# Neighbourhood attention inside a two-layer diffusion step: where the first output products, the context scores and the last heads' steps stand in the row of TensorE

## The chip, the cores and the metric

One core of one Trainium2 chip runs the whole program in a single launch. The time is the device time of one execution in microseconds (us), and the smaller is the better. The kernel before the change took 1602.42 us in the median of three runs (1601.96 to 1604.28).

## What is computed

The reference is one inference step of a trunk with two layers, on 128 context tokens ("prompt") and 512 latent tokens of width 1024, laid out as a grid of 8 rows of 64. Each layer is a token mixer followed by a gated feed-forward network with a width-3 convolution. The mixer of layer 0 is neighbourhood attention with 16 heads of 64, that of layer 1 is grouped-query attention. All arithmetic is float32. The part that the change touches, cut to its core:

```python
def na_qkv(h, w_qkv):                       # one product, split into queries, keys, values
    q, k, v = jnp.split(h @ w_qkv, 3, axis=-1)
...
qp, kp, vp = na_qkv(hp, na_w_qkv[i])        # the 128 context tokens
op = blocked_attention(qp, kp, vp)          # context attends to itself only
...
qs, ks_, vs = na_qkv(hs, na_w_qkv[i])       # the 512 latent tokens
os_ = neighbourhood_attention(qs, ks_, vs, cache_na_k[:, i], cache_na_v[:, i], na_rpb[i])
...
xp = xp + g_ap * rmsnorm(op.reshape(bp, tp, -1) @ w_o, norm_mix_post[l])
xs = xs + g_as * rmsnorm(os_.reshape(bs, ts, -1) @ w_o, norm_mix_post[l])
```

In neighbourhood attention a latent query sees the latent keys of all 8 rows within a window of 16 columns, with a learned relative bias, and all 128 cached context keys, in one softmax.

## The kernel before, in words

**Precision.** Every operand of a product is split into a high and a low part (`wh`/`wl` for weights, `oh`/`ol`, `kh`/`kl`, and so on), and a product is three matmuls: high by high, low by high, high by low. The splitting is a cast on ScalarE (ACT) for the high part and a subtraction on VectorE (DVE) or GpSimd (POOL) for the low one.

**One order for TensorE.** The helpers `mm` and `turn` (lines 113 to 117) tie each matmul and transpose to the one before it, so TensorE (PE) runs exactly in the order in which the program is written. The other engines' instructions are put in order by a scheduler when the program is built. Each engine then works through its own list first in, first out.

**Head 0 to head 15.** `Head.scores(slot)` (line 900) makes the scores of one of four blocks of 128 latent queries of one head: two matmuls into a PSUM bank `s`, on DVE the table of biases added with the running minimum (line 910), on ACT the exponential into `p` (line 914), on DVE the reciprocal `rc` of its sum (line 917), and on POOL `p` times `rc` (line 918). `Head.turns(i)` (line 920) transposes four 128x128 blocks of `p` on PE into a bank `tp` and copies them out as `pk`. `turns(0)` needs blocks of all four slots: its first two transposes those of slots 0 and 1, its third and fourth those of slots 2 and 3. `values` (line 934) multiplies two heads' transposed probabilities with the values, into the bank `po`. The bias table `tb` of a head is built on POOL by three subtractions (line 875), two heads' tables being kept at a time.

For the 128 context tokens, `prompt_scores` (line 637) makes the scores of four heads at once (eight matmuls of 128x128 into `sp`), with their exponentials `pp` on ACT and the scaling on POOL (line 658). `prompt_turn` (line 661) transposes them and copies them out as `ptp` on ACT (line 666). This is done in heads 1, 5, 9 and 13 for the heads of their group of four.

**The stream of other products.** `work` is a generator (line 978, `stream`) of pieces of the query, key and value products of later heads; each `fill()` takes one piece, that is 6 matmuls `qk` or 6 to 9 `vp`. When a pair's last key product is in, `kp` is transposed and written out by `tail` (line 846, bank `tk`). After head 12 the stream is empty, and `early` (line 1067) puts another in its place: pieces of the mixer's output product, each one `Mix.part0(t, p)` (line 701): three matmuls `y` of 128x512 that add the contribution of head pair `p` to the first 512 output columns of token block `t`. Head pair `p` needs `oh`/`ol`, the split of the attention's result (`o_split`, line 958). The pairs 0 and 1 (`OEARLY` is 2) are split after head 11, the pairs 2 to 5 after head 12, and 6 and 7 behind that.

**The tables.** Which step follows which inside a head is written out by hand in `ORDER` and `ORDER2` (lines 49 to 56), read by the loop at line 1012. `ORDER[0]` serves the even heads up to 12, `ORDER[1]` the odd ones up to 11, and `ORDER2` the heads 13 (index 1), 14 and 15. In a table `f` takes the next piece of `work`, `t0` to `t2` are this head's transposes, `s0` to `s3` the scores of the next head, `v` the values of two heads, `p0` to `p2` the scores, transposes and values of the context (only in heads 1, 5, 9 and 13), and `a` a step of the adaLN rows. `PRO` (line 57) is the number of pieces that are done ahead of head 0's scores.

**After the last head** the remaining output products follow, their normalization, and the first feed-forward network (`ffn`, line 1098), then layer 1. Its up-projection's weights are partly sums and differences (`wr`, lines 1167 to 1170, on DVE), which are split by ACT and POOL (lines 1146 and 1147), and its convolution runs on DVE (line 1223) and ACT (line 1221).

Of the kernel before, what the change touches and what calls it, by code (L numbers as in the profile page):

```python
# [2 lines left out]

# [21 lines left out]
NT = T // P  # L25
# [17 lines left out]
OEARLY = 2  # L43
# [2 lines left out]
NC = 3  # L46
QKH = (slice(0, 256), slice(256, T))
CTX = 2
ORDER = (
    "f f t0 s0 f s1 t1 f f t2 f a f f s2 s3 f f f f f f".split(),  # L50
    "f f p0 t0 s0 f s1 t1 f t2 p1 f f f v a p2 s2 s3 f f f".split(),
)
ORDER2 = (
    "t0 s0 s1 f f f f t1 f f t2 f f f s2 f f s3 f f f".split(),
    "t0 p0 s0 s1 f f f f t1 t2 p1 f f f v p2 s2 f s3 f f".split(),
)
PRO = 19
PSTEP = (3, 5, 6, 6, 8, 9)
WU = 29
TP = 1  # L60
# [41 lines left out]
def hybrid_step(ctx: ExitStack, tc: tile.TileContext, A, O):  # L102
# [10 lines left out]
    def mm(*a, **k):  # L113
        pe(nc.tensor.matmul(*a, **k))  # L114

    def turn(*a, **k):
        pe(nc.tensor.transpose(*a, **k))  # L117
# [4 lines left out]
    def pool(name, bufs=1, side="left", **k):  # L122
        return tc.tile_pool(name=name, bufs=bufs, side=side, reuse_waits="tile", **k)
# [187 lines left out]
    def drain(gen):  # L311
        for _ in gen:
            pass
# [347 lines left out]
    def prompt_turn(ap, pp, tag, nb):  # L661
        tp = bk.get("tp")
        for i in range(4):
            turn(tp[:, i * P : i * P + P], pp[:, i, :], ident)
        x = ap.tile([P, 512], F32, tag=tag, name="ptp", bufs=nb)
        nc.scalar.copy(x, tp)
        bk.put(tp)
        return x.rearrange("p (a b) -> p a b", a=4)
# [71 lines left out]
    with l_na:  # L740
# [39 lines left out]
        def na_qk_items(p):  # L780
# [13 lines left out]
            def k_put(c0, c1, src):  # L794
                for b in range(2):
                    own, oth = own_oth(b)
                    nc.scalar.copy(d["kh"][b][own, c0:c1], src[own])
                    nc.scalar.copy(d["kh"][b][oth, c0:c1], src[own])
                    nc.vector.tensor_sub(d["kl"][b][own, c0:c1], src[own], f32(d["kh"][b][own, c0:c1]))

            def part(which, half, k0):
# [27 lines left out]
                else:  # L829
                    if half == 0:  # L830
# [3 lines left out]
                        turn(tk[:, 0:P], d["kc"], ident)  # L834
                        k_put(CTX * P, CTX * P + P, tk[:, 0:P])
                        bk.put(tk)
                    if half == 1:
                        d["kp"] = ap.tile([P, P], F32, tag="kc", name="kp", bufs=2)
                        nc.scalar.copy(d["kp"], pp[:, NS - cs.start : T - cs.start])
                    k0 = cs.start + P * (cs.start >= CTX * P)  # L840
                    k_put(k0, k0 + nq, pp[:, 0:nq])
# [92 lines left out]
        def values(two):  # L934

            po = bk.get("po")
            vt = vts_of[two[0].h // 4]

            def block(ov, c, x):
                for v in two:  # L940
                    rows_ = slice(64 * v.b, 64 * v.b + 64)
                    mm(ov[rows_], vt[:, c, v.h % 4, :], x(v), start=c == 5, stop=c == 3)

            block(po, 5, lambda v: v.t[0])
            for i in (1, 2):
                for a, c in enumerate(Head.BANKS[i]):
                    ov = po[:, c * P : c * P + 256] if c < 3 else po.rearrange("p (a b) -> p a b", b=P)[:, 0::3, :]
                    block(ov, c, lambda v: v.t[i][:, a * 256 : a * 256 + 256])
            om = of0[two[0].h // 2][:, 0:NS].rearrange("p (r c) -> p r c", c=GW)
            for c0, c1, q0 in ((8, 56, 128), (56, 64, 0), (0, 8, 64)):  # L950
                nc.scalar.copy(om[:, :, c0:c1].rearrange("p r c -> p c r"),
                               po[:, q0 : q0 + 8 * (c1 - c0)].rearrange("p (c r) -> p c r", r=8))
            bk.put(po)

        osp0 = []
        m0 = Mix(0, A["na_w_o"][0], lambda p, t: tuple(x[:, t * P : t * P + P] for x in osp0[p]))

        def o_split(p):
            hi, lo = osp0[p]
            nc.scalar.copy(hi, of0[p])  # L960
            nc.vector.tensor_sub(lo, of0[p], f32(hi))
# [16 lines left out]
        def stream():  # L978
            items[0][0]()
            tail = None  # L980
            for n, (load, parts) in enumerate(items):
                for i, part in enumerate(parts):
                    part()
                    if n + 1 == len(items) and i in OW:
                        m0.weights(0, OW[i], None if i == 4 else nc.gpsimd)
                    if i == 1 and n + 1 < len(items):
                        items[n + 1][0]()
                    if i == 4 and tail:
                        tail()
# [12 lines left out]
        def fill(n=1):  # L1002
            for _ in range(n):
                next(work, None)

        fill(PRO)
        next(ada0)
        head = Head(0)
        for slot in range(4):
            head.scores(slot)  # L1010
            fill()
        for h in range(H):
            nxt = Head(h + 1) if h + 1 < H else None
            g = h // 4
            pr = h % 4 == 1
            order = (ORDER if h < 13 else ORDER2)[h % 2]
            for i, step in enumerate(order):
                if step == "f":
                    if i < len(order) - 1 or h % 4 or not h:
                        fill()  # L1020
                elif step == "a":
                    next(ada0, None)
                elif step[0] == "s" and nxt:
                    nxt.scores(int(step[1]))
                elif step[0] == "t":
                    head.turns(int(step[1]))
                elif step == "v":
                    values((before, head))
                if pr and step == "p0":
                    sides = []  # L1030
                    for hh in range(4 * g, 4 * g + 4):
                        qs, kh, kl = qk_of[hh // 2]
                        b = hh % 2
                        sides.append((qs[b][:, QW - P :], kh[b][:, T:], kl[b][:, T:]))
                    pp = prompt_scores(ap, sides)
                if pr and step == "p1":
                    pth = prompt_turn(ap, pp, "pk", NPK)
                if pr and step == "p2":
                    po = bk.get("po")
                    for j in range(2):  # L1040
                        for b in range(2):
                            mm(po[64 * b : 64 * b + 64, j * P : j * P + P], vts_of[g][:, 4, 2 * j + b, :],
                               pth[:, 2 * j + b, :], start=True, stop=True)
                    for j in range(2):
                        nc.scalar.copy(of0[2 * g + j][:, NS:T], po[:, j * P : j * P + P])
                    bk.put(po)
            before = head
            head = nxt
            if h == 11:
                drain(ada0)  # L1050
                l_ada.close()
                epool = l_na.enter_context(pool("o0e", 1))
                osp0.extend([epool.tile([P, T], F32R, name=f"o{i}{p}") for i in "hl"] for p in range(OEARLY))
                for p in range(OEARLY):
                    o_split(p)
            if h == 12:
                drain(work)
                r_h0.close()
                hpool = r_na.enter_context(pool("o0h", 1, "right"))
                osp0.extend([hpool.tile([P, T], F32R, name=f"o{i}{p}") for i in "hl"] for p in range(OEARLY, KC))  # L1060
                for p in range(OEARLY, 4):
                    o_split(p)
                m0.weights(0, 3)
                for p in range(4, 6):
                    o_split(p)

                def early():
                    for ts in (range(2), range(2, NT)):
                        for p in range(6):
                            for t in ts:  # L1070
                                m0.part0(t, p)
                                yield

                work = early()
            if h == 13:
                o_split(6)
        drain(work)
# [781 lines left out]
```

## Time and profile before

One execution was profiled; its own time is 1601.92 us, with 1600.1 us of it in the span that the profile shows.

| What | Value |
|---|---|
| Median of three runs | 1602.42 us |
| Profiled execution, time / span | 1601.92 / 1600.1 us |
| Busy share of the span: PE, DVE, ACT, POOL | 96%, 64%, 54%, 44% |
| PE: matmuls, busy | 9709, 1537.8 us |
| Mean granted clock of PE | 0.983 of full speed |
| Neighbourhood attention, head 0's first scores to head 15's values | about 82.6 to 349.9 us |

A row of the list of waits reads: engine, destination and line, the instruction that released it, then the idle time in all, how many times, and the longest. A row of the timeline reads: start in us, length in us (neighbouring instructions with the same names are put together, with their count behind the x), engine, line, operation, destination and sources, shape, and in brackets the idle time of the engine just before it and what ended that. A matmul's length holds its passage through the array, so neighbouring rows overlap; the distance from start to start is what it takes in a row of them. In a table of windows, each row has the stretch, its length, the busy time and number of instructions of PE, of its weight loads, of DVE, ACT and POOL, then the granted clock of PE (1.00 is full speed), the share of time in which the DMA engines were busy, and GB/s.

### The profile page before, as it was taken

The numbers are of one execution on the slowest core, as the hardware profiler recorded it, in microseconds if no ns is written. First come the engines' busy times: TensorE is split into PE (matmuls) and PEld (weight loads), VectorE is DVE, ScalarE is ACT, GpSimd is POOL, SyncE is SP. The second block draws the span as 40 slices with busy tenths as digits, with TensorE's granted clock in tenths as the row PEclk, the third lists the DMA queues.
The fourth block names the chain that finished last, engine by engine and source line by source line (L and its number), as shares of the span: only waits on it lengthen the run. The fifth ranks groups of instructions, "written<-read, shape, count | busy, mean of one in ns | idle before, by whom it ended". The sixth has DMA issues, their size and how long they took to land.

```text
span 1600.1 us, 26043 instructions
## 1 busy us (share of the span) xinstructions
PE 1537.8 (96%) x9709; PEld 1357.3 (85%) x9709; DVE 1023.9 (64%) x1650; ACT 859.8 (54%) x1641; POOL 710.9 (44%) x609
## 2 busy tenths in 40 slices
PE   5999999899999999999999898999999999999998
PEld 3989899778999999988887676777899999998886
DVE  3453533638877666665656867773787888876454
ACT  3474655545555555554453536764656565565343
POOL 1654544423255445534444344441324655553433
PEclk8999999899999999999999998999999999999999
DMA  9745454227466566578573110003644333348664
GB/s 288 188 112 146 115 156 117 65 69 234 140 197 203 195 211 184 188 255 288 169 238 132 60 40 14 2 1 106 234 125 158 117 114 108 105 158 269 207 213 139
DMA packets 193210, 242.41 MB, mean 151 GB/s; under 512 B 11100, under 2 KB 149564, under 8 KB 193084
## 3 DMA queue, kind: packets, MB, share of 16 engines
q1 hardware_dynamic: 182224, 233.13, 45.4%
q10 hardware_dynamic: 10860, 7.62, 2.7%
q8 instruction: 76, 1.25, 0.3%
q14 instruction: 50, 0.41, 0.1%
HBM read 214.38 MB, written 26.34 MB: 150 GB/s over the span
## 4 chain that ended last, share of the span: by engine, by line
PE 55%; DVE 9%; POOL 5%; ACT 3%; issue 3%; DMA 1%; ACTq 0%; POOLq 0%; DVEq 0%
PE acc L114 18%; PE ux L114 15%; PE uz L114 6%; PE uy L114 4%; PE y L114 2%; PE s L114 2%; PE po L114 2%; PE tp L117 2%; PE ada L114 2%; POOL wl L1147 1%; DVE t L1223 1%; POOL vl L1147 1%; DVE al L1147 1%; POOL rh L1467 1%; DVE wl L167 1%
## 5 line engine op out<-in xcount | busy, mean ns | idle before, releaser
L167 POOL TENSOR_TENSOR wl<-wr,wh 128x1024 fp32r<-128x1024 f32 x74 | 183.1, 2476 | 261.7 <-ACT wh L165 252.3
L1147 POOL TENSOR_TENSOR wl<-wr,wh 128x1024 fp32r<-128x1024 f32 x76 | 183.5, 2437 | 39.5 <-ACT wh L1146 35.9
L114 PE MATMUL ux<-B,wh 128*128 128x322 f32 x832 | 199.9, 311 | 0.7 <-ACT u L1200 0.7
L1223 DVE SCALAR_TENSOR_TENSOR t<-C,cw,t 128x644 f32<-128x644 f32 x176 | 156.3, 888 | 56.0 <-ACT t L1221 55.6
L114 PE MATMUL acc<-wh,alo 128*128 128x512 f32 x440 | 172.3, 392 | 0.5 <-DVE alo L1116 0.5
L114 PE MATMUL acc<-wh,ahi 128*128 128x512 f32 x440 | 172.0, 391 | 0.0
L114 PE MATMUL acc<-wl,ahi 128*128 128x512 f32 x440 | 171.9, 391 | 0.0
L165 ACT CAST wh<-wr 128x1024 fp32r<-128x1024 f32 x140 | 145.3, 1048 | 40.7 <-DMA wr<-in_ffn_w_down 30.9
L114 PE MATMUL uz<-B,wh 128*128 128x322 f32 x640 | 156.2, 312 | 0.7 <-ACT v L1200 0.7
L114 PEld LDWEIGHTS ux<-B,wh 128*128 128x128 f32 x832 | 143.4, 189 | 3.2 <-ACT u L1200 1.0
L1116 DVE TENSOR_TENSOR alo<-ain,ahi 128x384 fp32r<-128x384 f32 (+1 forms) x88 | 80.3, 930 | 85.7 <-ACT ahi L1114 84.7
L114 PE MATMUL ux<-B,wl 128*128 128x322 f32 x416 | 129.3, 311 | 2.7 <-DVE wl L1147 2.7
L114 PE MATMUL qk<-hT,wh 128*128 128x384 f32 (+1 forms) x512 | 122.9, 317 | 0.1
L114 PEld LDWEIGHTS uz<-B,wh 128*128 128x128 f32 x640 | 111.2, 189 | 3.6 <-ACT vh L1146 1.6
L1221 ACT ACTIVATE t<-C,cw 128x644 f32<-128x644 f32 x88 | 78.6, 894 | 53.8 <-DVE C L1251 41.1
L1147 POOL TENSOR_TENSOR vl<-wr,vh 128x1024 fp32r<-128x1024 f32 x38 | 96.3, 2534 | 24.6 <-ACT vh L1146 24.3
L1146 ACT CAST wh<-wr 128x1024 fp32r<-128x1024 f32 x84 | 84.9, 1049 | 40.9 <-DVE wr L1170 40.5
L167 DVE TENSOR_TENSOR wl<-wr,wh 128x1024 fp32r<-128x1024 f32 x66 | 86.9, 1329 | 22.6 <-ACT wh L165 22.0
L114 PE MATMUL uz<-B,wl 128*128 128x322 f32 x320 | 99.5, 311 | 0.0
L114 PEld LDWEIGHTS acc<-wh,alo 128*128 128x128 f32 x440 | 82.5, 188 | 19.1 <-DVE alo L1116 1.4
L114 PEld LDWEIGHTS acc<-wl,ahi 128*128 128x128 f32 x440 | 82.6, 188 | 17.8
L114 PEld LDWEIGHTS acc<-wh,ahi 128*128 128x128 f32 x440 | 82.6, 188 | 17.8
(251 smaller groups left out, 3965.3 us busy)
## 6 DMA issues: line engine op xcount, KB each, us to landing
wr<-in_ffn_w_up SPq DMA_DIRECT2D x88, 512.0 KB
wr<-in_ffn_w_down SPq DMA_DIRECT2D x88, 512.0 KB
wr<-in_ada_w SPq DMA_DIRECT2D x80, 512.0 KB
act<-act SPq DMA_DIRECT2D x44, 321.0 KB
wr<-in_na_w_qkv SPq DMA_DIRECT2D x24, 512.0 KB
mod<-modrow SPq DMA_DIRECT2D x20, 512.0 KB
ain<-act SPq DMA_DIRECT2D x44, 192.0 KB
wf<-in_ada_w SPq DMA_DIRECT2D x16, 512.0 KB
```

Source lines behind the costliest of these rows:

```text
L114: pe(nc.tensor.matmul(*a, **k))
L117: pe(nc.tensor.transpose(*a, **k))
L165: i = nc.scalar.copy(hi, raw)
L167: j = (low or nc.vector).tensor_sub(lo, raw, f32(hi))
L1116: pin(nc.vector.tensor_sub(lo[:, 0 : c1 - c0], ain[:, 0 : c1 - c0], f32(hi[:, 0 : c1 - c0])))
L1146: nc.scalar.copy(hl[0], src)
L1147: low.tensor_sub(hl[1], src, f32(hl[0]))
L1221: nc.scalar.activation(t, taps(0), AF.Identity, bias=cw[:, 3, n : n + 1], scale=cw[:, 1, n : n + 1])
L1223: nc.vector.scalar_tensor_tensor(t, taps(d), cw[:, w, n : n + 1], t, op0=ALU.mult, op1=ALU.add)
L1467: last_rms[0] = nc.gpsimd.tensor_tensor(r, v, mhalf.broadcast_to([P, n]), op=ALU.pow)
```

## The change

Four things are moved; no product, no transfer and no buffer is added or taken away. PE has the same matmuls and transposes.

1. **Head 0.** One piece more of `work` stands ahead of its first scores (`PRO` 20 in place of 19), none behind its fourth score (`fill(slot < 3)`), and its own table `ORDER0` has one `f` more in front and one fewer at the end.
2. **Heads 1, 5 and 9.** The context's scores `p0` come first in the head, ahead of the two pieces that stood before them.
3. **From head 12 to head 13.** When head 11 is done, four pieces of the output product (token blocks 0 and 1, pairs 0 and 1) are chained behind the stream of key products. Head 12's last `f` steps, which had nothing left to hand out but `tail`, hand these out.
4. **Heads 13, 14 and 15.** `ORDER2` is written anew: head 13 starts with `p0 s0 s1` and has `t0` behind them; in heads 13 and 14, `s2` and `s3` come further ahead of the end of the head, with more pieces behind them.

```diff
+from itertools import chain
...
+ORDER0 = "f f f t0 s0 f s1 t1 f f t2 f a f f s2 s3 f f f f f".split()
 ORDER = (
     "f f t0 s0 f s1 t1 f f t2 f a f f s2 s3 f f f f f f".split(),
-    "f f p0 t0 s0 f s1 t1 f t2 p1 f f f v a p2 s2 s3 f f f".split(),
+    "p0 f f t0 s0 f s1 t1 f t2 p1 f f f v a p2 s2 s3 f f f".split(),
 )
 ORDER2 = (
-    "t0 s0 s1 f f f f t1 f f t2 f f f s2 f f s3 f f f".split(),
-    "t0 p0 s0 s1 f f f f t1 t2 p1 f f f v p2 s2 f s3 f f".split(),
+    "t0 s0 s1 f f f t1 f f t2 f s2 f s3 f f f f f f f".split(),
+    "p0 s0 s1 t0 f f f t1 f t2 f s2 p1 f s3 v p2 f f f f".split(),
 )
-PRO = 19
+PRO = 20
...
         for slot in range(4):
             head.scores(slot)
-            fill()
+            fill(slot < 3)
...
-            order = (ORDER if h < 13 else ORDER2)[h % 2]
+            order = (ORDER if h < 13 else ORDER2)[h % 2] if h else ORDER0
...
             if h == 11:
+                def early(ps, *rows_):
+                    for ts in rows_:
+                        for p in ps:
+                            for t in ts:
+                                m0.part0(t, p)
+                                yield
+
+                work = chain(work, early(range(OEARLY), range(2)))
...
-                work = early()
+                work = chain(early(range(OEARLY, 6), range(2)), early(range(6), range(2, NT)))
```

Three places in the engines' lists, word for word. Line numbers behind the change are two higher at the helpers and three higher behind the loop over the heads.

The first place is PE's list at the end of head 12. The transposes `tp<-ident,p` there are head 13's `t0`, `tk` is the last key product's transpose, `sp` the context's scores, and the `s` matmuls at the end are head 14's first scores. Before:

```order
L114 MATMUL s<-kh_2941,qs_2780 128x384
L114 MATMUL s<-kl_616,qs_2780 128x384
L117 MATMUL tk<-ident,kp 128x128
L117 MATMUL tp<-ident,p 128x128 x4
L114 MATMUL sp<-kh_2940,qs_2779 128x128
L114 MATMUL sp<-kl_615,qs_2779 128x128
L114 MATMUL sp<-kh_3508,qs_3337 128x128
```

And in the changed kernel, from the same two score matmuls (head 13's fourth block):

```order
L116 MATMUL s<-kh_2941,qs_2780 128x384
L116 MATMUL s<-kl_616,qs_2780 128x384
L119 MATMUL tk<-ident,kp 128x128
L116 MATMUL y_3591<-wh,oh_3423 128x512
L116 MATMUL y_3591<-wl,oh_3423 128x512
L116 MATMUL y_3591<-wh,ol_3424 128x512
L116 MATMUL y_3595<-wh,oh_3423 128x512
L116 MATMUL y_3595<-wl,oh_3423 128x512
L116 MATMUL y_3595<-wh,ol_3424 128x512
L116 MATMUL y_3591<-wh,oh_3425 128x512
```

Five more `y` matmuls follow there, then the eight `sp`, four `s` for head 14's first two blocks, and only then the four transposes `tp` of head 13. So 12 + 8 + 4 matmuls that stood behind those transposes now stand ahead of them.

The second place is POOL's list at the start of the attention. `tb_611` is rebuilt there for head 2 while head 0 runs, and `p<-p,rc` scales head 0's four blocks of probabilities. Before:

```order
L875 TENSOR_TENSOR tb_611<-mask,tr 128x2x128
L875 TENSOR_TENSOR tb_611<-mask,tr 128x256
L918 TENSOR_SCALAR p<-p,rc 128x384 x2
L875 TENSOR_TENSOR tb_611<-mask,tr 128x256
L918 TENSOR_SCALAR p<-p,rc 128x384 x2
```

And in the changed kernel:

```order
L877 TENSOR_TENSOR tb_611<-mask,tr 128x2x128
L920 TENSOR_SCALAR p<-p,rc 128x384
L877 TENSOR_TENSOR tb_611<-mask,tr 128x256
L920 TENSOR_SCALAR p<-p,rc 128x384
L877 TENSOR_TENSOR tb_611<-mask,tr 128x256
L920 TENSOR_SCALAR p<-p,rc 128x384 x2
```

The first two scalings moved ahead of one or two of the table's subtractions, and the last two stand behind the last subtraction as before.

The third place is DVE's list early in the first feed-forward network. `wr` are the sums and differences of weights, `t` is the convolution. The scheduler's order differs here although the code does not. Before:

```order
L1147 TENSOR_TENSOR al<-wr,ah 128x512
L1167 TENSOR_TENSOR wr<-wr 128x512
L1168 TENSOR_TENSOR wr<-wr 128x512
L1169 TENSOR_TENSOR wr<-wr 128x512
L1170 TENSOR_TENSOR wr<-wr 128x512
L1223 SCALAR_TENSOR_TENSOR t<-C,cw_83,t 128x2x322 x3
```

And in the changed kernel:

```order
L1150 TENSOR_TENSOR al<-wr,ah 128x512
L1226 SCALAR_TENSOR_TENSOR t<-C,cw_83,t 128x2x322
L1170 TENSOR_TENSOR wr<-wr 128x512
L1226 SCALAR_TENSOR_TENSOR t<-C,cw_83,t 128x2x322
L1171 TENSOR_TENSOR wr<-wr 128x512
L1172 TENSOR_TENSOR wr<-wr 128x512
L1173 TENSOR_TENSOR wr<-wr 128x512
```

Two convolution steps have moved ahead of the weights' sums. In the next few units the two kinds are interleaved differently as well, and behind that the two lists agree again. PE's list is the same in both kernels from head 15's values to the end.

More of the change, by code (lines that the diff above doesn't have):

```diff
@@ L1065, in hybrid_step @@
                     o_split(p)
[L1067 to L1072, printed above, removed]
-                work = early()
+                work = chain(early(range(OEARLY, 6), range(2)), early(range(6), range(2, NT)))
             if h == 13:
```

## The prediction, put on record ahead of the run

> **What bounds the kernel now.** I read the page's busy times first, then the list of PE's waits, then the timeline and a table of windows at the places that the change touches. The page's first section:
>
> ```profile
> PE 1537.8 (96%) x9709; PEld 1357.3 (85%) x9709; DVE 1023.9 (64%) x1650; ACT 859.8 (54%) x1641; POOL 710.9 (44%) x609
> ```
>
> PE is busy for 1537.8 of 1600.1 us, and the change takes no matmul away. It can only win from PE's waits and from the stretches in which its clock is halved. The list of PE's waits has these lines that the change touches:
>
> ```profile
> PE tp L117 <- POOL p L918: 6.2, 3, 4.4
> ...
> PE s L114 <- ACT kh L798: 1.5, 1, 1.5
> PE tp L117 <- POOL pp L658: 1.3, 3, 0.4
> ...
> PE s L114 <- DVE kl L799: 0.2, 1, 0.2
> ```
>
> That is 9.2 us of idle time in all. The clock adds to it, as PE's timeline at the end of head 12 shows:
>
> ```profile
> 304.38 0.38 PE L117 MATMUL tp<-ident,p 128*128 128x128 f32 x2
> 309.16 0.47 PE L117 MATMUL tp<-ident,p 128*128 128x128 f32 x1 [4.40 <-POOL p L918]
> 310.29 0.48 PE L117 MATMUL tp<-ident,p 128*128 128x128 f32 x1 [0.65 <-POOL p L918]
> 310.42 0.46 PE L114 MATMUL sp<-kh,qs 128*128 128x128 f32 x1
> ...
> 313.55 0.63 PE L114 MATMUL y<-wh,oh 128*128 128x512 f32 x1
> ...
> 317.25 0.40 PE L114 MATMUL y<-wl,oh 128*128 128x512 f32 x1
> 317.48 0.41 PE L114 MATMUL y<-wh,ol 128*128 128x512 f32 x1
> 317.72 1.04 PE L117 MATMUL tp<-ident,p 128*128 128x128 f32 x8
> ```
>
> The third and fourth transposes of head 13's `t0` wait for the probabilities of its last two blocks. PE stands from 304.76 to 309.16, then goes on slowly. The granted clock says why; in this table of windows it is the number behind the five engines' columns:
>
> ```profile
> 84.50:86.00 1.50, 1.50 (x6) 1.50 (x5) 1.22 (x4) 1.47 (x3) 1.50 (x1) 0.50 0.05 11
> 87.50:89.00 1.50, 1.50 (x9) 1.50 (x9) 1.16 (x5) 0.68 (x3) 0.53 (x1) 0.88 1.02 292
> 310.30:316.30 6.00, 6.00 (x20) 5.42 (x21) 4.44 (x10) 3.31 (x14) 0.23 (x1) 0.50 0.30 87
> 400.40:404.00 3.60, 3.58 (x24) 3.57 (x25) 3.60 (x4) 1.26 (x2) 0.00 (x0) 1.00 0.50 148
> ```
>
> The clock is 0.50 throughout 310.30 to 316.30, behind the long wait, and again around 84.5 to 87.9 in head 0. (In the second row, 0.88 means that the slow part ends about 0.36 us into that window: it lasts some 3.4 us, from 84.5 to 87.9.) It stays at 1.00 behind the wait of 1.40 us at 400.42, whose row stands further below.
>
> **Term C, the handover from head 12 to 13: −7.3 us.** The scaled probabilities come from a chain on three other engines:
>
> ```profile
> 306.92 0.58 ACT L914 ACTIVATE p<-s,nm 128x384 f32<-128x384 f32 x1
> 307.49 0.57 ACT L914 ACTIVATE p<-s,nm 128x384 f32<-128x384 f32 x1
> ...
> 306.32 1.66 POOL L875 TENSOR_TENSOR tb<-mask,tr 128x256 f32<-128x256 f32 x2 [3.04 <-DVE nm L910]
> 307.98 2.25 POOL L918 TENSOR_SCALAR p<-p,rc 128x384 f32<-128x384 f32 x2
> ```
>
> Nothing in the change makes this chain faster: in ACT's, DVE's and POOL's lists the same casts and exponentials stand ahead. I take the two blocks as ready when PE used them before, at about 309.1 and 310.2. In between PE now has work: 12 `y` at 0.23 us from start to start (317.25 to 317.48) are 2.8 us; the eight `sp` and four `s` took 313.55 − 310.42 = 3.1 us at half clock, so about 1.6 at full. From 304.4, behind `tk`, that reaches to 308.8. Two transposes more, and PE waits about 0.1 us for the third block and 0.9 for the fourth. `t0` ends at about 310.4, with all done that before was done at 317.72, a gain of 7.3: some 4 us of idle time and some 3.2 of half clock. The second is at risk with the first: were the remaining wait to lower the clock again, half of it would go (a rival, below). Bounds: 5.9 if the exponentials slip by 1.4 us because ACT and DVE now serve the context's scores sooner; 8.2 if the remaining wait vanishes.
>
> Are the early `y` ready? Their pairs 0 and 1 were split after head 11, and their weights are the same that the `y` at 313.55 used without a wait. They need two free PSUM banks some 9 us sooner than before; on PE's list the first product there waits for no other engine. I price this at nothing. Cover gone, it would cost the 2.8 us that they fill.
>
> **Term D, head 14's `t0`: −1.7 us.** There the fourth transpose waits as well:
>
> ```profile
> 327.28 0.82 PE L117 MATMUL tp<-ident,p 128*128 128x128 f32 x3
> 329.25 0.33 PE L117 MATMUL tp<-ident,p 128*128 128x128 f32 x1 [1.15 <-POOL p L918]
> 329.33 0.43 PE L114 MATMUL s<-kh,qs 128*128 128x384 f32 x1
> ...
> 332.90 0.60 PE L117 MATMUL tp<-ident,p 128*128 128x128 f32 x4
> 333.26 0.48 PE L114 MATMUL y<-wh,oh 128*128 128x512 f32 x1
> ```
>
> Four transposes take 333.26 − 332.90 = 0.36 us unhindered, and 329.33 − 327.28 = 2.05 here. The new table has `s3`, the head's values, `p2` and four pieces between, over 6 us of PE work in place of two pieces (six `y`, 1.4 us), so the wait goes; what is late next there is nothing that the trace shows. Bounds 1.2 (the idle time alone) to 1.7.
>
> **Term B, the context scores ahead in heads 1, 5 and 9: −2.0 us.** PE's timeline in head 1:
>
> ```profile
> 113.37 0.60 PE L117 MATMUL tp<-ident,p 128*128 128x128 f32 x4
> 114.39 0.65 PE L117 MATMUL tp<-ident,pp 128*128 128x128 f32 x4 [0.41 <-POOL pp L658]
> ```
>
> Four transposes pass in 0.36 us and the next starts 1.02 later: 0.66 lost, three times (the waits' line has 3 of 0.4), so 2.0. `p0` moves ahead by two pieces, 12 matmuls or about 2 us, which is more than the wait. The keys that `p0` reads come out of the last piece ahead of it, so a new wait for their casts may take a part back: bounds 1.2 (the idle time alone) and 2.0.
>
> **Term A, head 0: −1.2 us.** Its scores wait for the keys' casts:
>
> ```profile
> 82.64 0.44 PE L114 MATMUL s<-kh,qs 128*128 128x384 f32 x1 [1.46 <-ACT kh L798]
> 83.32 0.41 PE L114 MATMUL s<-kl,qs 128*128 128x384 f32 x1 [0.23 <-DVE kl L799]
> ...
> 91.31 1.14 POOL L918 TENSOR_SCALAR p<-p,rc 128x384 f32<-128x384 f32 x2
> ...
> 91.91 0.93 PE L117 MATMUL tp<-ident,p 128*128 128x128 f32 x4
> ```
>
> Six matmuls took 1.50 us at half clock (84.50 to 86.00), so a piece at full clock is 0.75, and that much of the 1.46 is filled. The remaining idle time, 0.7 + 0.23, is less than the 1.40 us that left the clock at 1.00 at 400.42, so the low stretch of about 3.4 us should go, which is worth 1.7. That makes 2.4. But the transposes at 91.91 then come at 90.2, while POOL's last two scalings still stand behind the last piece of a table and ended at 92.45: between 0 and 2.2 us of new wait, since the scores come sooner too. I take the middle, 1.2 of wait, and 1.2 of gain; bounds 0.2 and 2.4.
>
> A rule that speaks against half of this term is in the Trainium skill (TensorE: Matmul & The Clock Gate, "Why this matters for your kernels"): it asks for no idle gap of more than about 3 us. By it a gap of 1.69 us wouldn't have lowered the clock, the low stretch would stay, and the sum below would be 10.1; it is the first rival.
>
> **New waits: +0.4 us.** Two things queue anew in head 13. First, ACT's copy `ptp` now stands behind four exponentials of head 14 in place of two, and `p2` waits for it. Second, the context's transposes `p1` wait for POOL's `pp`, which needs DVE's reciprocal behind these rows:
>
> ```profile
> 311.89 1.22 DVE L167 TENSOR_TENSOR wl<-wr,wh 128x1024 fp32r<-128x1024 f32 x1
> 313.02 1.55 DVE L961 TENSOR_TENSOR ol<-of,oh 128x640 fp32r<-128x640 f32 x2
> ```
>
> Worked forward from the moved `sp`, `pp` is ready at about 314.5 and PE arrives at about 314.8; `ptp` at about 318.1 against 318.9. Both are close, so 0 to 1.5 us, and I take 0.4.
>
> **The sum.** 7.3 + 1.7 + 2.0 + 1.2 − 0.4 = 11.8 us. Everything behind 349.9 us is the same list on PE, started sooner. The profiled execution (1601.92, with 1600.1 of span) would become 1590.1; it stands 0.5 under the median, and the median of 1602.42 becomes 1590.6. The bounds: 5.9 + 1.2 + 1.2 + 0.2 − 1.5 = 7.0, or 1595.4; and 8.2 + 1.7 + 2.0 + 2.4 = 14.3, or 1588.1.
>
> **The rivals.** The stage behind the attention matters for two of them:
>
> ```profile
> 349.80:387.00 37.20, 37.20 (x176) 30.68 (x175) 27.61 (x39) 23.89 (x53) 14.08 (x25) 1.00 0.73 241
> 387.00:420.00 33.00, 31.60 (x216) 30.95 (x214) 31.23 (x38) 19.20 (x36) 6.87 (x11) 1.00 0.31 97
> ```
>
> The timeline there shows PE's one wait and, later, POOL's split of two weights (`wl`) and PE's first use of them; the page's row has DVE's convolution:
>
> ```profile
> 400.42 0.41 PE L114 MATMUL ux<-B,wl 128*128 128x322 f32 x1 [1.40 <-DVE wl L1147]
> ...
> 427.55 4.76 POOL L1147 TENSOR_TENSOR wl<-wr,wh 128x1024 fp32r<-128x1024 f32 x2 [4.12 <-ACT wh L1146]
> ...
> 437.09 0.31 PE L114 MATMUL ux<-B,wl 128*128 128x322 f32 x1
> ```
>
> ```profile
> L1223 DVE SCALAR_TENSOR_TENSOR t<-C,cw,t 128x644 f32<-128x644 f32 x176 | 156.3, 888 | 56.0 <-ACT t L1221 55.6
> ```
>
> *The low stretch of head 0 stays* whatever the gap: 1.7 less, 1592.3. For it: only two cases show what lowers the clock. Against it: both have an idle time of over 1.6 us just ahead, and shorter ones have none. Chance 0.10.
>
> *The clock falls again at head 13's `t0`*, the 1.0 us of remaining wait being drawn out to 1.7 by slower exponentials: 0.7 and half of 3.4 us lost, 2.4 less, 1593.0. Chance 0.10.
>
> *The gain is given back before 420 us.* The loads for the feed-forward network keep the DMA engines busy for 0.73 of 349.8 to 387, and DVE works 31.23 of the next 33 us. If they can't start sooner, PE's wait at 400.42 grows: with three quarters of 11.8 lost, 1599.5. Against it: PE has no idle time at all from 349.8 to 387, and the loads are let go by buffers that PE and ACT free, so they move with PE. Chance 0.08.
>
> *The feed-forward network becomes slower.* DVE's list puts two convolution steps of 0.888 us ahead of the weights' sums, so POOL's `wl` comes 1.8 us later. It decides from the point at which that exceeds the lead: the two end near 429.9 and at 432.31, and the first is used at 437.09, so even the second's end leaves 4.8 us. If the lag grew over the 22 units instead, at 1.2 each, 26 us would be added: 1617. Chance 0.04, since the lists agree again a few units on.
>
> *The change doesn't do what it says*: the early products wait for a free bank until the old place of `t0`, and only the 1.6 us of `sp` and `s` fill the gap. C is 1.6 in place of 7.3, the sum 6.1: 1596.3. On PE's list nothing but a bank's release stands ahead of them, so 0.05.
>
> **How the numbers follow.** The forecast has 0.63, and its time is 1590.6. The range from 1588.0 to 1597.5 takes in the bounds, the first two rivals and the last, and leaves out the third and fourth, 0.12 together, and what surprises there are. About 0.2% (3.2 us) is what a measurement can tell from no change. Faster: 0.63 + 0.20 + 0.05 = 0.88; same is the third rival's 0.08 (1599.5 is 2.9 us under the median); slower 0.04.
>
> **What would show it.** Right: `y` matmuls directly behind `tk`, no wait over 1.4 us for `p` at head 13, a clock of 1.00 from 300 to 350 us, the waits for `pp` gone from the list, and head 15's values some 11 us sooner, with the same distance from there to the end. A clock of 0.50 behind `t0`, or a new wait for `pp` or `ptp` in head 13, would show the terms mis-sized; a PE wait at 400.42 of several us would show the third rival, and waits of `ux` for `wl` all along the first network the fourth.

## The result, and the profile after

The changed kernel takes 1588.49 us in the median of four runs (1587.89 to 1589.93), the kernel before, run beside it, 1603.1 us (1601.96 to 1604.28, four runs). The ratio is 0.991, with a 95% interval of 0.9893 to 0.9927: 14.6 us faster, where 11.8 were forecast. The profiled execution took 1588.34 us, with a span of 1586.5.

The page's first section has the same work on PE, done in 10.8 us less of busy time, since less of it ran at half clock (about half of that lies in the parts that the change touches, as shown below):

```profile
PE 1527.0 (96%) x9709; PEld 1350.0 (85%) x9709; DVE 1023.6 (65%) x1650; ACT 862.1 (54%) x1641; POOL 712.2 (45%) x609
```

The list of PE's waits, cut to the lines that the prediction named and one that is new:

```profile
PE tp L119 <- POOL p L920: 1.1, 2, 0.9
...
PE po L116 <- DVE qs L827: 0.8, 3, 0.3
...
PE s L116 <- ACT kh L800: 0.7, 1, 0.7
...
PE s L116 <- DVE kl L801: 0.2, 1, 0.2
```

The wait for the scaled probabilities `p` fell from 6.2 to 1.1 us and that for the keys' casts from 1.5 to 0.7. The waits for the context's `pp` are gone from the list; in their place the values' products (`po`) wait three times for the queries' split. PE's timeline at the handover from head 12 to 13:

```profile
300.63 0.33 PE L119 MATMUL tk<-ident,kp 128*128 128x128 f32 x1 [0.21 <-ACT kp L841]
300.71 0.48 PE L116 MATMUL y<-wh,oh 128*128 128x512 f32 x1
...
303.59 0.22 PE L116 MATMUL sp<-kh,qs 128*128 128x128 f32 x1
...
304.44 0.40 PE L116 MATMUL s<-kh,qs 128*128 128x384 f32 x1
...
305.19 0.78 PE L119 MATMUL tp<-ident,p 128*128 128x128 f32 x3
306.85 0.33 PE L119 MATMUL tp<-ident,p 128*128 128x128 f32 x1 [0.87 <-POOL p L920]
306.93 0.48 PE L116 MATMUL y<-wh,oh 128*128 128x512 f32 x1
```

The 12 `y` take 2.88 us, the eight `sp` 0.85, the four `s` 0.75, and 0.87 us of wait are left. The table of windows has the granted clock at 1.00 in head 0 and through the whole handover:

```profile
84.50:86.00 1.50, 1.50 (x11) 1.47 (x10) 0.84 (x2) 1.45 (x4) 1.50 (x1) 1.00 0.05 12
300.60:305.20 4.60, 4.57 (x26) 3.99 (x27) 4.25 (x10) 4.51 (x12) 2.46 (x3) 1.00 0.66 241
307.00:334.00 27.00, 27.00 (x151) 21.68 (x151) 11.39 (x33) 11.08 (x35) 5.83 (x11) 1.00 0.11 39
```

In the stretch of 84.50 to 86.00, PE now works on 11 matmuls where it worked on 6.

**Where the time went.** I cut both timelines at four places where the same work stands behind PE: the first key and query product, head 2's first transposes, head 12's first transposes, and head 15's values. In the kernel before:

```profile
64.60 0.28 PE L114 MATMUL qk<-hT,wh 128*128 128x256 f32 x1
...
127.84 0.27 PE L117 MATMUL tp<-ident,p 128*128 128x128 f32 x1
...
294.27 0.60 PE L117 MATMUL tp<-ident,p 128*128 128x128 f32 x4
347.12 2.81 PE L114 MATMUL po<-pk,vt 128*64 128x512 f32 x20
```

And in the changed one:

```profile
65.06 0.28 PE L116 MATMUL qk<-hT,wh 128*128 128x256 f32 x1
...
125.57 0.27 PE L119 MATMUL tp<-ident,p 128*128 128x128 f32 x1
...
290.68 0.60 PE L119 MATMUL tp<-ident,p 128*128 128x128 f32 x4
334.56 2.81 PE L116 MATMUL po<-pk,vt 128*64 128x512 f32 x20
```

The differences of these starts, with those of the experiments below (each from its own timeline; "end" is the span):

| Part of the span, us | before | after | a_head0 | b_ctx | cd_tail | again |
|---|---|---|---|---|---|---|
| start to first `qk` (not touched) | 64.60 | 65.06 | 66.71 | 66.33 | 64.52 | 66.65 |
| to head 2's first transposes | 63.23 | 60.51 | 61.03 | 62.91 | 63.63 | 60.62 |
| to head 12's first transposes | 166.44 | 165.11 | 166.12 | 165.51 | 166.48 | 165.10 |
| to head 15's values | 52.85 | 43.88 | 52.23 | 53.08 | 43.89 | 43.84 |
| to the end (same list on PE) | 1252.98 | 1251.94 | 1253.2 | 1253.7 | 1252.1 | 1252.5 |

The three middle rows, all of PE's list that the change touches, give 2.72 + 1.33 + 8.97 = 13.0 us of the profiled 13.6. The rest, −0.5 and +1.0, lies in the first and the last row. The windows over the three middle rows together, first before and then after, split the 13.0:

```profile
64.60:347.12 282.52, 271.38 (x1968) 242.80 (x1966) 119.68 (x346) 156.32 (x423) 133.46 (x142) 0.98 0.42 108
65.06:334.56 269.50, 265.48 (x1969) 238.75 (x1967) 118.93 (x345) 157.18 (x423) 134.02 (x142) 1.00 0.43 113
```

PE is busy 5.9 us less, at a clock of 1.00 in place of 0.98, and idle for 4.0 us in place of 11.1. So 7.1 us come from waits and 5.9 from the clock. The other 4.9 of the 10.8 us of busy time lie in the untouched first and last rows, where the slow stretches fell otherwise.

### The profile page after: what moved, and what is told of

Its sections match the earlier page's. It is cut to its first block, busy times and chain, and to the rows that moved or that the text cites. A ratio compares the mean times of both kernels' runs of the same rounds, so it can differ in the third digit from the quotient of the medians.

```text
span 1586.5 us, 26049 instructions
## 1 busy us (share of the span) xinstructions
PE 1527.0 (96%) x9709; PEld 1350.0 (85%) x9709; DVE 1023.6 (65%) x1650; ACT 862.1 (54%) x1641; POOL 712.2 (45%) x609
## 3 DMA queue, kind: packets, MB, share of 16 engines
q8 instruction: 76, 1.25, 0.3%
## 4 chain that ended last, share of the span: by engine, by line
PE 57%; DVE 8%; POOL 5%; ACT 3%; issue 3%; DMA 1%; ACTq 0%; POOLq 0%; DVEq 0%
PE acc L116 18%; PE ux L116 16%; PE uz L116 7%; PE uy L116 4%; PE y L116 2%; PE s L116 2%; PE po L116 2%; PE tp L119 2%; PE ada L116 2%; POOL wl L1150 1%; POOL vl L1150 1%; DVE t L1226 1%; POOL rh L1470 1%; DVE al L1150 1%; DVE wl L169 1%
```

## The experiments

Every kernel computes all that the reference does. Times are medians against the kernel before on the same chip; the parts named are those of the table.

### a_head0: the part of head 0 alone

```diff
+ORDER0 = "f f f t0 s0 f s1 t1 f f t2 f a f f s2 s3 f f f f f".split()
-PRO = 19
+PRO = 20
-            fill()
+            fill(slot < 3)
-            order = (ORDER if h < 13 else ORDER2)[h % 2]
+            order = (ORDER if h < 13 else ORDER2)[h % 2] if h else ORDER0
```

> The head-0 part alone (one piece more ahead of the first scores, none behind the fourth, the table of its own). Theory 1, filled idle time plus a full clock: the wait for the casts of the keys is 0.74 us in place of 1.46, the clock stays at 1.00 from 84 to 88 us, and the time falls by 2.2 us (0.72 + 1.7, less 0.2 of new wait for the scaled probabilities at the first transposes). Theory 2, gaps under 3 us don't act on the clock: the low stretch of 3.4 us behind these scores is still there and the time falls by 0.5 us at most.

Measured: 1599.3 us against 1603.8, ratio 0.9972 (0.9961 to 0.9982). In the trace the part up to head 2 fell from 63.23 to 61.03 us and the next by 0.3. The windows of this run:

```profile
82.70:86.00 3.30, 2.32 (x15) 1.89 (x15) 1.27 (x3) 3.18 (x8) 0.15 (x1) 1.00 0.79 182
86.00:89.40 3.40, 3.40 (x22) 3.36 (x21) 2.39 (x8) 3.31 (x7) 3.08 (x2) 1.00 0.04 12
```

About 1.0 us of 3.30 is idle, and the clock stays at 1.00. The mechanism is theory 1's; 2.2 to 2.5 us of gain can be placed. The medians differ by 4.5, and the 2 us between are not found in the parts that the edit touches; the profiled execution (1601.08 us) was the slowest of the seven (1597.45 to 1601.08). The handover from head 12 to 13, which this edit leaves as it was, took 52.23 us in place of 52.85, with a slow stretch of 6.83 us (from 307.90) in place of 10.24 (from 306.31): what the old handover costs differs by itself from execution to execution.

### b_ctx: the context scores at the front of heads 1, 5 and 9 alone

```diff
-    "f f p0 t0 s0 f s1 t1 f t2 p1 f f f v a p2 s2 s3 f f f".split(),
+    "p0 f f t0 s0 f s1 t1 f t2 p1 f f f v a p2 s2 s3 f f f".split(),
```

> The context scores at the front of heads 1, 5 and 9 alone. Theory 1: the three waits of 0.4 us for the scaled context probabilities are gone from TensorE's list, 0.63 us each from start to start, and the time falls by 1.9 us. Theory 2, given back: the waits go, but what stands behind waits as much longer (the values' bank or the queries' casts), and the time falls by less than 0.5 us.

Measured: 1603.33 us against 1603.8, ratio 0.9995 (0.9987 to 1.0004): not told from no change. The trace has the three waits for `pp` gone and 0.32 + 0.93 = 1.25 us less in the two parts; a new wait of about 0.25 us stands ahead of each of the three `po`. So some of the gain is given back, and the trace lies between theory 1's 1.9 and theory 2's 0.5. The profiled execution was nonetheless slower than that of before, since its first row took 66.33 us in place of 64.60.

### cd_tail: the early products and the new tables of heads 13 to 15

The edit is the two `work = chain(...)` hunks with `early`, and `ORDER2`, from the change's diff.

> The early output products with the new tables of heads 13 to 15, and neither of the other two parts. Theory 1: as in the whole change, some 0.9 us of wait is left at head 13's first transposes, the clock stays at 1.00 from 300 to 350 us, the wait of head 14 is gone, and the time falls by 9.0 us (7.2 + 1.8). Theory 2, the parts depend on each other (a shift of the 3.4-us grid of the clock lets it fall behind the 0.9 us): the time falls by 7.0 us or less, with a clock of 0.50 behind the transposes.

Measured: 1594.58 us against 1603.8, ratio 0.9948 (0.9936 to 0.9961), 9.2 us less. The part from head 12 to head 15's values took 43.89 us, as in the whole change (43.88): 8.96 less, theory 1. Head 0's slow stretch is still there, since nothing was done about it:

```profile
80.60:83.90 3.30, 1.34 (x9) 0.91 (x8) 1.34 (x4) 3.18 (x8) 0.00 (x0) 1.00 0.80 184
84.00:87.30 3.30, 3.30 (x14) 3.29 (x13) 1.83 (x5) 3.26 (x7) 3.10 (x2) 0.50 0.03 8
```

Here 1.96 of 3.30 us are idle, and the next stretch runs at 0.50.

### d_order2: the new tables without the early products

The edit is `ORDER2` alone.

> The new tables of heads 13 to 15 alone: the output products start only behind head 12, as before. Between the transposed key and head 13's first transposes stand the context scores and two blocks of scores, 1.6 us at full clock. Theory 1: some 3 us of wait are left there, the clock falls to 0.50 as before, and the time falls by 1.6 + 1.8 = 3.4 us (3.0 to 4.5). Theory 2, it is the moved scores and tables that bring the gain and the early products only follow along: the time falls by 6 us or more.

Measured: 1597.8 us against 1603.8, ratio 0.9963 (0.995 to 0.9977). The part to head 15's values took 48.65 us, 4.20 less than before, which is theory 1's size. The medians, though, differ by 6.0, which is theory 2's. The six executions lie between 1594.89 and 1601.13 us, with a mean clock of 0.988 to 0.981, and the profiled one is the slowest of them; what this part took in the others is not known, so the size is left open between the two theories. How the gain came was not what I had expected. The wait for `p` is all but gone (0.34 us here), and new waits of 1.6 us stand in the context scores, since PE comes to them before the casts of the last keys are done:

```profile
PE sp L114 <- ACT kh L798: 1.0, 2, 0.6
PE sp L114 <- DVE kl L799: 0.6, 2, 0.4
```

The clock then fell for two stretches of 3.4 us, from 311.8 to 318.6, behind a stretch (308.40 to 311.80) in which PE was idle for 1.28 us.

### c_early: the early products with the old tables

The edit is the two `work = chain(...)` hunks with `early` alone.

> The four early output products alone, with the old tables of heads 13 to 15: the 12 matmuls stand behind the last key product, and head 13's first transposes right behind them. From head 12's first transposes to head 15's values the kernel before took 52.85 us (10.2 of them at half clock) and the whole change 43.88. Theory 1: 2.8 of the 4.8 us are filled, some 2.6 us of wait are left, the clock still falls for at least one stretch of 3.4 us, head 14's wait stays: 48 to 50 us for this part, and 3 to 5 us less in all. Theory 2, the early products do it all and the tables only tidy up: 45 us or less.

Measured: 1599.38 us against 1603.39, ratio 0.9976 (0.9967 to 0.9985). The part took 48.31 us, 4.54 less than before. 2.4 us of wait for `p` were left (1.64 and 0.80), cut in two by the clock's grid (the 3.4-us stretches of the last section), and the clock stayed at 1.00: here theory 1 was wrong, though its size held. A wait of 0.82 us for `pp` is new in head 13. Theory 2 was wrong by more. In the two profiled executions the halves alone give 4.54 and 4.20, together 8.74 of the 8.97: each brings about half there.

### n2: two early products in place of four

```diff
-                work = chain(work, early(range(OEARLY), range(2)))
+                work = chain(work, early(range(1), range(2)))
-                work = chain(early(range(OEARLY, 6), range(2)), early(range(6), range(2, NT)))
+                work = chain(early(range(1, 6), range(2)), early(range(6), range(2, NT)))
```

> The whole change with two early output products (pair 0) in place of four; the other two come behind head 12. Six matmuls less in the gap lengthen the wait at head 13's first transposes from 0.87 us to about 2.25 us in all. Theory 1, about 1.7 us of idle time within one stretch of the clock's grid is enough: the clock falls for 3.4 us, and the part from head 12's first transposes to head 15's values takes 43.88 + 1.4 + 1.7 = 47.0 us where it falls, 45.3 where the wait is cut in two by the grid. Theory 2, gaps under 3 us don't act on the clock: 45.3 us always, with a clock of 1.00.

Measured: 1591.05 us against 1603.39, ratio 0.9925 (0.991 to 0.994). The part took 46.09 us, and the clock fell there:

```profile
302.20:305.60 3.40, 2.17 (x12) 1.50 (x11) 3.05 (x9) 3.38 (x8) 3.20 (x4) 1.00 0.53 171
305.70:309.00 3.30, 3.30 (x10) 2.52 (x10) 3.30 (x7) 3.30 (x13) 0.00 (x0) 0.50 0.05 3
```

Theory 2 falls: 1.23 us without a matmul in one stretch were enough here, and they are four waits of 0.23 to 0.39 us, two in the context scores and two for `p`. The 47.0 of theory 1 was too much, because the wait for `p` was 0.56 us and not 2.25; POOL had the probabilities sooner than in the whole change. The next kernels say why. The size of the idle time alone doesn't decide: in c_early a stretch with 1.24 us of idle time left the clock at 1.00.

```profile
307.30:310.60 3.30, 2.06 (x10) 1.40 (x8) 2.95 (x10) 3.25 (x9) 2.49 (x3) 1.00 0.62 211
310.70:314.00 3.30, 2.21 (x15) 2.02 (x16) 2.03 (x3) 3.20 (x8) 1.36 (x2) 1.00 0.00 0
```

### n6: six early products

```diff
-                work = chain(work, early(range(OEARLY), range(2)))
+                work = chain(work, early(range(OEARLY), range(3)))
-                work = chain(early(range(OEARLY, 6), range(2)), early(range(6), range(2, NT)))
+                work = chain(early(range(OEARLY, 6), range(3)), early(range(6), range(3, NT)))
```

> The whole change with six early output products (pairs 0 and 1 of three token blocks) in place of four. Theory 1: the 0.87 us of wait that was left at head 13's first transposes is filled, and the part from head 12's first transposes to head 15's values takes 43.0 us. Theory 2, a third bank held that early makes the scores or the transposes wait for banks: the 0.87 us come back as waits elsewhere in heads 13 and 14, 43.9 us or more. In the whole time 0.9 us can hardly be told from nothing.

Measured: 1590.3 us against 1603.39, ratio 0.9919 (0.9905 to 0.9932). The part took 43.93 us: no gain, and for neither theory's reason. PE came to the transposes 1.4 us later after `tk`, and still waited 0.75 us for `p`. POOL's two scalings had become slower; its rows here and DVE's:

```profile
304.94 3.34 POOL L920 TENSOR_SCALAR p<-p,rc 128x384 f32<-128x384 f32 x2
...
304.62 1.02 DVE L963 TENSOR_TENSOR ol<-of,oh 128x640 fp32r<-128x640 f32 x1
...
305.72 1.05 DVE L963 TENSOR_TENSOR ol<-of,oh 128x640 fp32r<-128x640 f32 x1
306.69 1.21 DVE L169 TENSOR_TENSOR wl<-wr,wh 128x1024 fp32r<-128x1024 f32 x1
```

Elsewhere two scalings take 1.16 us. DVE's subtractions (`ol`, `wl`), with both operands in SBUF, run during nearly all of POOL's 3.34. In n2, where one `ol` ran beside them, the two took 1.69, and in the whole change, where two did, 2.35:

```profile
304.44 2.35 POOL L920 TENSOR_SCALAR p<-p,rc 128x384 f32<-128x384 f32 x2
...
304.13 1.00 DVE L963 TENSOR_TENSOR ol<-of,oh 128x640 fp32r<-128x640 f32 x1
305.06 0.15 DVE L919 RECIPROCAL rc<-su 128x1 f32<-128x1 f32 x1
...
305.58 0.84 DVE L963 TENSOR_TENSOR ol<-of,oh 128x640 fp32r<-128x640 f32 x1
```

That was a theory by then, and the next two kernels test it.

### n4_low and n6_low: DVE's subtractions moved out of POOL's way

The same edit, in the whole change and in n6: the `ol` of the pairs 2 to 5 are taken out of `o_split` and stand behind the context scores' minima, and the last weights are split behind head 13's second transposes.

```diff
+                if h == 13 and step == "t1":
+                    m0.weights(0, 3)
+                if h == 13 and step == "s0":
+                    for p in range(OEARLY, 6):
+                        nmp_last[0] = behind(o_low(p), nmp_last[0])
...
-                    o_split(p)
+                    o_split(p, False)
-                m0.weights(0, 3)
```

> The whole change, with DVE's low parts (ol) of the pairs 2 to 5 moved behind the context scores' minima, and the split of the last weights (wl) behind head 13's second transposes, so that DVE does no subtraction while POOL scales head 13's last two blocks. Theory 1, the 0.87 us of wait that was left come from POOL being slowed by DVE's subtractions at the same time (two scalings took 2.35 us there, and 1.16 elsewhere): they take about 1.2 us now, the wait falls to 0.2 or less, and the part from head 12's first transposes to head 15's values takes 43.2 us in place of 43.88. Theory 2, the scalings are slow there for another reason (their own waits for DVE's reciprocals): 2.3 us as before, and 43.9 us.

> The same move of DVE's subtractions in the kernel with six early output products, where two scalings took 3.34 us and 0.75 us of wait stayed although 1.4 us more work covers it. Theory 1: about 1.2 us for the two, no wait for them, and 43.0 us for the part from head 12's first transposes to head 15's values. Theory 2, another reason: 3.3 us, a wait of 0.75, 43.9 us.

Measured: n4_low 1588.82 us against 1602.1, ratio 0.9917 (0.9904 to 0.9931); n6_low 1589.45, ratio 0.9921 (0.9908 to 0.9933). POOL in n4_low, and what became of PE's wait:

```profile
304.32 1.15 POOL L923 TENSOR_SCALAR p<-p,rc 128x384 f32<-128x384 f32 x2
...
305.11 0.74 PE L119 MATMUL tp<-ident,p 128*128 128x128 f32 x4
...
306.74 0.50 PE L116 MATMUL y<-wh,ol 128*128 128x512 f32 x1 [0.42 <-DVE ol L971]
```

The two scalings take 1.15 us in both kernels, against 2.35 and 3.34: theory 1 on the cause. The move also brings DVE's second reciprocal sooner, to 304.52, but theory 2 can't be the reason: in the whole change that reciprocal was done at 305.21, while POOL was at its first scaling until 305.59. Head 13's transposes don't wait; the `y` behind them wait 0.42 us for the subtraction that was moved. The part took 43.63 and 43.28 us, 0.25 and 0.65 less than with four and six products before the move, where 0.7 and 0.9 were expected. In the whole time neither is told from the change.

### best: one piece more ahead of head 0's scores

This is n6 with:

```diff
-PRO = 20
+PRO = 21
-ORDER0 = "f f f t0 s0 f s1 t1 f f t2 f a f f s2 s3 f f f f f".split()
+ORDER0 = "f f f t0 s0 f s1 t1 f f t2 f a f f s2 s3 f f f f".split()
```

> As the kernel with six early output products, with one piece more ahead of head 0's scores (21, and one fewer at the head's end). Theory 1: the wait for the casts of the keys (0.74 us) is filled as well, so the stretch from the first key and query product to head 2's first transposes takes 59.8 us in place of 60.51, and the whole 1.6 us less than the change. Theory 2, the scaled probabilities come no sooner, and the wait at head 0's first transposes grows from 0.23 us by what was filled: 60.5 us.

Measured: 1596.65 us against 1603.39, ratio 0.9966 (0.9954 to 0.9979), 6 us more than n6. The wait for the keys' casts is gone, as expected, but the part to head 2's transposes took 68.77 us in place of 60.99. The scheduler had put a split of weights on POOL between head 0's third and fourth scaling:

```profile
90.74 1.71 POOL L920 TENSOR_SCALAR p<-p,rc 128x384 f32<-128x384 f32 x3
92.42 0.84 POOL L877 TENSOR_TENSOR tb<-mask,tr 128x256 f32<-128x256 f32 x1
93.23 2.33 POOL L169 TENSOR_TENSOR wl<-wr,wh 128x1024 fp32r<-128x1024 f32 x1
95.55 0.58 POOL L920 TENSOR_SCALAR p<-p,rc 128x384 f32<-128x384 f32 x1
```

PE's timeline and the clock behind it:

```profile
96.19 0.47 PE L119 MATMUL tp<-ident,p 128*128 128x128 f32 x1 [3.35 <-POOL p L920]
```

```profile
95.30:101.90 6.60, 5.45 (x20) 4.99 (x21) 3.16 (x11) 3.62 (x12) 2.04 (x4) 0.50 0.46 110
```

3.35 us of wait and 6.6 us at half clock; in head 1 PE then waits 1.04 and 1.40 us for the queries' split. Neither theory foresaw this: the scaled probabilities came later, where theory 2 had them come no sooner. A piece more ahead of the scores moved POOL's list here, and that decided.

### again: the changed kernel once more

> The changed kernel once more, as it is, beside the two others on the same chip. If the phase of the clock's grid of 3.4 us differs from execution to execution, the parts that no edit touches (the start up to the first key and query product, and layer 1's mixer) take other times than in its first profile by up to 2.5 us, while the part from head 12's first transposes to head 15's values stays at 43.9 us and the one from the first key and query product to head 2's transposes at 60.5 us. If the phase is fixed for a kernel, all of them repeat within 0.2 us.

Measured: 1590.53 us against 1602.1, ratio 0.9923 (0.9911 to 0.9935). The touched parts repeat within 0.11 us (60.62, 165.10, 43.84); the part ahead of them took 66.65 us in place of 65.06. The same stretch of both executions, first this one, then the changed kernel's first:

```profile
62.10:65.40 3.30, 3.30 (x15) 3.30 (x16) 0.00 (x0) 0.87 (x3) 3.09 (x6) 0.50 0.31 99
```

```profile
62.10:65.40 3.30, 3.30 (x28) 3.30 (x29) 0.00 (x0) 1.62 (x5) 3.10 (x6) 1.00 0.44 127
```

PE runs at 0.50 here and at 1.00 there, on the same list. Of the 2.2 us between the two spans, 1.6 lie ahead of the first `qk` and 0.6 in the last row. A change of 1 to 2 us therefore has to be read from the trace's parts.

## Why the prediction was right, point by point

**The forecast** of 1590.6 us lay 2.1 above the measured median, and the range held it by 0.5 us at its low end, with one of the four executions (1587.89) below it. Where 11.8 us of gain were forecast, the trace places 13.0 in the touched parts, and the 1.0 us of the last row, which scatters by itself, helped the median down. That the sum came so near is in part luck: term A and the pair of D and the new waits brought about 1.0 and 0.5 us more than forecast, term B 0.75 less.

**Term C, 7.3 us.** From head 12's first transposes to the end of head 13's `t0`, with the same work done, it was 317.72 − 294.27 = 23.45 us and is 306.93 − 290.68 = 16.25: 7.20. The mechanism, the cover and the 0.9 us of wait left are as forecast, and the clock stayed at 1.00. One step was right by luck: I took POOL's 2.25 us for two scalings as the length of the chain. Half of it was DVE's subtractions (the two scalings take 1.15 us without them), which the moved work happened to leave in place; n6 showed that more cover brought nothing while they stood there.

**Term D, 1.7, and the new waits, 0.4.** From there to head 15's values it was 347.12 − 317.72 = 29.40 us and is 334.56 − 306.93 = 27.63: 1.77. D was right; the new waits for `pp` and `ptp` did not come. With the old tables the one for `pp` did (0.82 us in c_early), so the price was not for nothing.

**Term B, 2.0.** The three waits for `pp` went, and b_ctx places 1.25 us. The prediction took the upper of its bounds, 1.2 and 2.0, and looked for a new wait at the keys' casts; it came at the values, where `po` waits 0.25 us three times for the queries' split.

**Term A, 1.2.** Its part brought 2.2 us (a_head0), near my upper bound of 2.4. The step that failed is the new wait at `t0`, taken as 1.2: it is 0.23, because POOL's list has the last piece of the table out of the way sooner:

```profile
89.76 0.88 POOL L877 TENSOR_TENSOR tb<-mask,tr 128x256 f32<-128x256 f32 x1
90.61 1.16 POOL L920 TENSOR_SCALAR p<-p,rc 128x384 f32<-128x384 f32 x2
```

The table ends 0.7 us earlier than before, though the first `qk` started 0.46 us later, and the fourth scaling ends at 91.77 in place of 92.45.

**The rivals.** The slow stretch of head 0 did not stay. The rule that it was set against asks for no idle gap over about 3 us (the Trainium skill, TensorE: Matmul & The Clock Gate, "Why this matters for your kernels"). It is no safe bound here: cd_tail's clock fell behind a stretch with 1.96 us of idle time and n2's behind one with 1.23, in which no single gap was over 0.39 us, while a_head0's 0.98 left it alone. The clock did not fall at head 13's `t0`; with two early products it did. Nothing was given back before 420 us: PE's wait for the first network's weights is 1.41 us, and stands 12.56 us sooner, just as head 15's values do.

```profile
387.86 0.42 PE L116 MATMUL ux<-B,wl 128*128 128x322 f32 x1 [1.41 <-DVE wl L1150]
```

The first network's reordered steps on DVE cost nothing that can be seen: the last row of the table is 1.0 us shorter, not longer. I can't put that 1.0 us down to the change, since the same kernel gave 1251.9 and 1252.5 in two executions, and the two experiments that leave heads 13 to 15 as they were 1253.2 and 1253.7; n2 and n6, which have the new tables, took 1253.1 and 1253.2.

## What to carry to other kernels

Look for the place where the busiest engine waits and its clock then drops, and move work there that depends on nothing recent; price the wait and the slow stretch together, since the second can be nearly as large as the first. Before adding more cover, look at what the late producer itself waits for: here it shared its time with another engine's subtractions, and more cover only moved both. A shift by one piece can reorder a list on another engine that no line of the edit names, so the lists around the edit are read, not only the edited one.

## What the runs showed of the hardware that was not expected

- Half-clock stretches last about 3.4 us or a multiple, on a grid whose phase differs from execution to execution. In the kernel before they start at 84.45 and 306.31 us and last 3.41 and 10.24; the starts are 221.86 us apart, 65 times 3.413, and in each of the 13 profiled executions all such starts lie whole multiples of 3.413 us apart. The untouched start took 64.52 to 66.71 us in the six executions of the table.
- What lowers the clock is not one long gap. From 60 us on in these executions, no full-clock stretch of the grid with under 1.2 us of idle time in all lowered it, and every one with 1.9 us or more did. In between both occur: 1.23 (n2), 1.28 (d_order2) and 1.69 (head 0 before) lowered it; 1.33 (c_early, with 1.24 in the window shown) and 1.47 did not. The 1.47 are n6's, in head 0:

```profile
81.56:84.97 3.41, 1.94 (x12) 1.51 (x11) 1.27 (x3) 3.29 (x8) 0.29 (x1) 1.00 0.82 182
84.97:88.38 3.41, 3.41 (x22) 3.38 (x21) 2.56 (x8) 3.32 (x7) 3.04 (x3) 1.00 0.06 15
```

  What else counts, perhaps the kind of matmuls in a stretch, stays open.
- Two scalings on POOL took 1.15 us alone, 1.69 beside one DVE subtraction of two SBUF operands, 2.35 beside two, and 3.34 beside two, a split of weights and the start of a third. The Trainium skill (SBUF — State Buffer, "Who interferes with whom") says that a DVE instruction with two SBUF inputs contends with a GpSimd one that reads SBUF, and that the port pair which they share is an exclusive lock. The runs agree: in the kernel before, the whole change, n2 and n6, each slowed scaling ended 0.37 to 0.45 us behind the end of a DVE subtraction that ran beside it, where a scaling alone takes 0.58, so it did most of its work only when that was done. Moving the subtractions brought the 1.15 back.
